# A routed decoder block on one core: a re-ordered mixer, no branch ahead of the first expert, and branch values read together

## The chip, the cores and the metric

The kernel runs on one core of one Trainium2 chip, from one launch, with all inputs and the output in the core's HBM. The metric is device microseconds (us) of one execution; the number given is the median of three. Five engines work side by side: PE (matrix products; its weight loads are a second row, PEld), DVE and ACT (element-wise work), POOL (element-wise work and some DMA issues), and SP, which only issues DMAs. Each runs its own list of instructions in order and waits at semaphores for the others.

## What is computed

One decoder block over 256 tokens of width 1024, in float32. A token mixer with two branches (a short causal convolution, and a state-space scan with 32 heads in 4 groups) is followed by a channel mixer that sends each token to 4 of 32 experts. Cut to what matters here:

```
h = rms_norm(x) * (1 + sc1) + sh1                       # sh, sc, gt: silu(c) @ w_ada + b_ada, six rows
proj = h @ w_in -> sb, sc, sx, z, xbc, dt, gate_a, gate_b
y_a = (sc * conv3(sb * sx)) @ w_sconv_out
xs, bs, cs = split(silu(conv4(xbc) + b)); dt = softplus(dt + dt_bias); a = -exp(a_log)
y   = scan(xs, dt, a, bs, cs) + d_skip * xs             # over the 256 tokens
y_b = group_rms_norm(y * silu(z)) @ w_ssm_out           # 4 groups of 512
x   = x + gt1 * ((sigmoid(gate_a) * y_a + sigmoid(gate_b) * y_b) @ w_o)
h   = rms_norm(x) * (1 + sc2) + sh2
logits = h @ w_router + b_router                        # top 4 of 32, softmax over the 4
for each expert e, over the tokens sent to it:
    gate, up = h @ w_gu[e] + b_gu[e]
    out += weight * (((clip(up) + 1) * gate * sigmoid(1.702 * gate)) @ w_down[e] + b_down[e])
out = rms_norm(x + gt2 * out) * g_final
```

## The kernel before, in words

**The mixer.** `items` is a list of projections, each a product of a 1 MB weight with the 256 normalised tokens. A weight is split into a high and a low part (`split`, L189 to L191: ACT writes the high part, POOL or DVE subtracts to get the low one) and each product is done as three (`mm3`, L193 to L196). `add(load, engines, run)` registers an item and says which engine makes the low part of its two halves; `take()` (L224) hands out the next half and at the same time issues the splits of the halves up to three further on. The order is: dt (`run_dt`, L458), 4 convolution items for B and C (`conv_pair`, L498), 8 for xs, 8 for z (`run_z`), 12 for the short convolution (`run_sb`, `run_sx`, `run_sc`), two gates, 4 of `run_ya`, 8 of `run_yb`, 6 of `run_gate`, and the output product `w_out`. The scan is cut into steps; `ssd_step` (L666) runs the steps placed at the next position, two positions per item of z and of the short convolution. `group_norm(g)` (L627) sums squares on PE, takes a reciprocal root on DVE (`rsqrt_mean`) and returns a `finish` that spreads it over the rows by a PE product.

**The loop over items** (L941 to L953) runs an item, then what the item before it left in `later`, then the row steps that `rows_here` put there, then the item's `after` hooks. A row step (`row_step`, L357) adds one of 32 slices of `w_ada` into an accumulator on DVE (L362, L364); after 8 slices a row of modulation is complete and `total` (PE, L373) and `turn` follow, one item apart.

**The experts' weights** come in pieces of 2 MB, six an expert (four of `w_gu`, two of `w_down`), through a ring of ten places. `eissue(n)` (L99) issues the pieces up to number n. Most ring places are buffers of the mixer, so the first ten pieces start as the mixer lets go of them, and piece j + 10 when the expert that read piece j is done with it. PE, ACT, DVE and POOL keep the order of the program; the order of SP's queue is laid out by the program's own scheduler, since SP is not among the engines in `MANUAL`.

**The experts** run in pairs (`expert`, L1325; `last_pair`, L1339). Expert e takes up to 64 rows (`CAP`): products `gate_up` (L1194 biases, L1198), the activation on DVE and ACT, a turn, products `down` (L1224); the pair's output is weighted and added by `combine` (L1244, L1246). Rows 65 to 96 of an expert are done in branches. Between expert e and e + 1 stands a branch on the larger of the two counts (`cnt2`), and inside it two more on the count of each (`extra_down`, `extra_gate_up`). A branch is taken on PE, ACT and DVE, each of which loads the count into a register first (`rows_of`, L1306). Ahead of expert 0 stands a branch of its own, on its count (L1135, L1317). Any rows past 96 of an expert are done at the end by `leftover`, under a branch on the largest count (`cnt_max`, L1515).

## Time and profile before

| | |
|---|---|
| median of 3 runs | 1399.8 us (1398.98 to 1400.66) |
| the profiled execution, its own time | 1405.03 us |
| its span (first to last recorded instruction) | 1403.2 us |
| mean granted PE clock | 0.971 of full speed |
| PE busy | 1309.4 us (93%), 7417 products |
| DVE / ACT / POOL busy | 550.0 / 287.2 / 91.1 us |
| bytes read from HBM | 492.45 MB, mean 352 GB/s |

The mixer takes the span up to about 450 us, the experts the rest. A row of a timeline gives the start and the length in us, the engine, the line, the operation, and in brackets how long the engine had been idle before it and what ended that. `PEq`, `ACTq`, `SPq` are the engines' sequencers (branches, register loads, DMA issues). A busy PE is not PE at its peak: the same product is shorter at the full clock than at half of it.

### The profile page before, as it was taken

What the parts mean: (1) busy time and instruction counts of PE and PEld (TensorE: products, weight loads), DVE (VectorE), ACT (ScalarE), POOL (GpSimd) and SP (SyncE); (2) the same over time, 40 slices, a digit from 0 to 9 for tenths busy, and PEclk for the clock granted to TensorE, in tenths of its full rate; (3) what the DMA queues carried; (4) which work ended last, traced back from release to release, by engine and by line L of the source; (5) the groups of instructions that cost most, each with busy time, mean ns of one, the idle gap of its engine ahead of it and who ended that gap; (6) DMA issues with size and microseconds to landing.
All of it is one profiled execution on the core that took longest, in us unless ns stands there. A gap on an engine that the chain in (4) does not pass through costs nothing. (4 is left out here: it accounts for less than half of the span.)

```text
span 1403.2 us, 18018 instructions
## 1 busy us (share of the span) xinstructions
PE 1309.4 (93%) x7417; PEld 735.8 (52%) x7417; DVE 550.0 (39%) x1026; ACT 287.2 (20%) x440; POOL 91.1 (6%) x71
## 2 busy tenths in 40 slices
PE   4899999999988999999999999999989888999995
PEld 1899998899987344344333434434423233334432
DVE  1846788976744223213212322222321213221323
ACT  1657965454433000000000000000000000000002
POOL 3682000000022000000000000000000000000000
PEclk9899999999989999999999999999999998999998
DMA  9555545568977799999999999999999999999991
GB/s 363 219 193 182 196 180 191 182 234 306 360 271 282 315 422 426 425 426 425 425 426 427 426 425 424 428 423 426 425 426 425 425 426 427 417 393 426 428 409 69
DMA packets 47977, 495.46 MB, mean 353 GB/s; under 512 B 6640, under 2 KB 6768, under 8 KB 15200
## 3 DMA queue, kind: packets, MB, share of 16 engines
q1 hardware_dynamic: 46928, 492.48, 86.0%
q8 instruction: 97, 1.59, 0.5%
q0 software_dynamic: 624, 0.53, 0.1%
q10 hardware_dynamic: 288, 0.52, 0.1%
q14 instruction: 40, 0.33, 0.1%
HBM read 492.45 MB, written 1.06 MB: 352 GB/s over the span
## 5 line engine op out<-in xcount | busy, mean ns | idle before, releaser
L1198 PE MATMUL pgu<-ring,arena 128*64 128x512 f32 x1856 | 418.0, 606 | 9.3 <-DMA ring<-in_w_gu_dram 9.2
L1198 PEld LDWEIGHTS pgu<-ring,arena 128*64 128x64 f32 x1856 | 135.0, 139 | 275.7 <-issue 257.1
L1185 DVE TENSOR_SCALAR arena<-pgu 128x512 f32<-128x512 f32 x32 | 22.1, 692 | 512.4 <-PE pgu L1198 302.3
L1224 PE MATMUL py<-ring,arena 128*64 128x512 f32 x912 | 202.8, 596 | 0.7 <-ACTq L1354 0.7
L1186 ACT ACTIVATE pgu<-arena 128x512 f32<-128x512 f32 x32 | 19.3, 602 | 732.3 <-DVE arena L1185 732.3
L1224 PEld LDWEIGHTS py<-ring,arena 128*64 128x64 f32 x912 | 62.7, 137 | 126.7 <-issue 112.4
L191 DVE TENSOR_TENSOR parts<-arena,parts 128x1024 fp32r<-128x1024 f32 x76 | 93.5, 1238 | 46.7 <-ACT parts L190 46.6
L190 ACT ACTIVATE parts<-arena 128x1024 fp32r<-128x1024 f32 x94 | 97.8, 1050 | 56.2 <-issue 15.6
L1496 POOL TENSOR_TENSOR arena<-arena 128x512 f32<-128x512 f32 x2 | 2.5, 1270 | 946.0 <-DVE arena L1246 946.0
L1244 PE MATMUL pcm<-arena 128*128 128x512 f32 x128 | 61.7, 605 | 0.9 <-DVE arena L1474 0.9
L194 PE MATMUL pc<-slot_h,parts 128*128 128x256 f32 x192 | 56.3, 293 | 2.7 <-DVE arena L514 2.7
L196 PE MATMUL pc<-slot_h,parts 128*128 128x256 f32 x192 | 55.9, 291 | 2.9 <-POOL parts L191 2.9
L1158 PE MATMUL pgat<-arena 128*128 128x128 f32 x480 | 58.5, 275 | 0.0
L1474 DVE TENSOR_TENSOR arena<-py,arena 128x512 f32<-128x512 f32 x32 | 20.6, 686 | 95.4 <-PE py L1224 80.9
L1158 PEld LDWEIGHTS pgat<-arena 128*128 128x128 f32 x480 | 56.1, 192 | 0.0
L195 PE MATMUL pc<-slot_h,parts 128*128 128x256 f32 x192 | 55.7, 290 | 0.0
L1194 PE MATMUL pgu<-bgu 128*128 128x512 f32 x64 | 24.3, 462 | 27.9 <-PEq L1320 17.5
L191 POOL TENSOR_TENSOR parts<-arena,parts 128x1024 fp32r<-128x1024 f32 x18 | 45.5, 2536 | 73.3 <-DVE row_ebuf L364 43.8
L1198 PE MATMUL pgu<-arena 128*64 128x512 f32 x192 | 43.3, 593 | 1.0 <-DMA arena<-in_w_gu_dram 0.9
L514 DVE SCALAR_TENSOR_TENSOR arena<-pc,arena 128x253 f32<-128x253 f32 (+2 forms) x72 | 33.5, 481 | 23.0 <-ACT arena L509 21.3
L1246 DVE TENSOR_TENSOR arena<-arena,pcm 128x512 f32<-128x512 f32 x64 | 39.9, 680 | 1.1 <-PE pcm L1244 1.1
L196 PEld LDWEIGHTS pc<-slot_h,parts 128*128 128x128 f32 x192 | 38.2, 199 | 3.3 <-POOL parts L191 3.3
(342 smaller groups left out, 2041.0 us busy)
## 6 DMA issues: line engine op xcount, KB each, us to landing
ring<-in_w_gu_dram SPq DMA_DIRECT2D x116, 2048.0 KB, 27.1
ring<-in_w_down_dram SPq DMA_DIRECT2D x54, 2048.0 KB, 28.0
arena<-in_w_gu_dram SPq DMA_DIRECT2D x12, 2048.0 KB, 33.0
arena<-in_w_main_dram SPq DMA_DIRECT2D x23, 1024.0 KB, 5.6
row_ebuf<-in_w_ada_dram SPq DMA_DIRECT2D x32, 512.0 KB, 4.0
arena<-in_w_down_dram SPq DMA_DIRECT2D x6, 2048.0 KB, 31.5
ring_more<-in_w_main_dram SPq DMA_DIRECT2D x9, 1024.0 KB, 6.7
arena<-in_w_gate_dram SPq DMA_DIRECT2D x8, 1024.0 KB, 7.6
```

The source lines that it names most:

```text
L190: nc.scalar.activation(hi, src, AF.Copy)
L191: lo_engine.tensor_tensor(lo, src, hi, op=ALU.subtract)
L194: nc.tensor.matmul(dst, w[0], x[0], start=first, stop=False)
L195: nc.tensor.matmul(dst, w[0], x[1], start=False, stop=False)
L196: nc.tensor.matmul(dst, w[1], x[0], start=False, stop=last)
L514: nc.vector.scalar_tensor_tensor(ts[a][:, d:], pm[:, a, 0:T - d], v2t[:, col:col + 1], ts[a][:, d:], op0=ALU.mult, op1=ALU.add)
L1158: nc.tensor.matmul(pg[:, k], h2[:, tb, k0 + k], sel[:, tb], start=(tb == 0), stop=(tb == 1))
L1194: nc.tensor.matmul(pgu[i], bias_lhs(), bias_rhs(i), start=True, stop=False)
L1198: nc.tensor.matmul(pgu[q // 2][64 * hh:64 * hh + 64], xg[:, k, s0:s0 + CAP], w[k // 2][:, k % 2, 512 * q:512 * q + 512], start=False, stop ...
L1224: nc.tensor.matmul(outs[dh][64 * cg:64 * cg + 64], aT[:, q, 64 * h:64 * h + 64], w[h][:, q, 512 * dh:512 * dh + 512], start=(h == 0 and q ...
L1244: nc.tensor.matmul(pc, pwT[:, dh, tb], ysb[:, dh], start=True, stop=True)
L1246: nc.vector.tensor_tensor(o_acc[:, tb, sl], o_acc[:, tb, sl], pc, op=ALU.add)
```

## The change

It has three parts. In the mixer: small products of a unit matrix are put behind the last three `w_ada` products and behind the turn of the modulation (`idle_products`); the copy into `rcol` goes behind `make_h`; `run_dt` is cut into five parts of which four are run one item later each; the second convolution item gets one half's subtraction on DVE (`MIXED`); `turn_dt` goes from the first xs item to the sixth; `group_norm` and its `finish` get fixed positions; one row step leaves the last `run_sc` item, one each leaves the gates (1, 1) and (2, 1), and three more stand at `run_yb`; pieces 1 to 3 of the expert weights are issued one at a time behind the gates (1, 0), (2, 0) and (2, 1). Ahead of expert 0: the register load and the branch go; `cmax` is raised by 32 above expert 0's count, so that rows past 64 of expert 0 are left to `leftover`, which shifts expert 0's positions to match. At the other branches: the counts for the outer and the two inner branches are loaded together inside `down`, in front of the branch.

```diff
--- before.py
+++ after.py
@@ -314,6 +314,13 @@
 
     smod0 = at(40, [P, 512])
     pm0 = paux("pada0", [P, 512])
+
+
+    def idle_products(nm, n):
+        t = ptr(nm, [P, P])
+        for i in range(n):
+            nc.tensor.matmul(t, ident, ident, start=True, stop=True)
+
     xps = []
     for i in range(8):
         ada_mm(pm0, i, ada0[i])
@@ -323,10 +330,13 @@
             turn_small()
         if i == 3:
             turn_x()
+        if i >= 5:
+            idle_products(f"idle{i}", 3)
     nc.vector.tensor_tensor(smod0, pm0, badar, op=ALU.add)
     mcol_p = ptr("mcol_p", [P, 4, P])
     for q in range(4):
         nc.tensor.transpose(mcol_p[:, q], smod0[:, P * q:P * q + P], ident)
+    idle_products("idle8", 14)
 
     nc.vector.tensor_copy(mcol.rearrange("p r q -> p q r"), mcol_p[:, :, 0:P:32])
     mflat = mcol.rearrange("p r q -> p (r q)")
@@ -387,9 +397,6 @@
 
         later.append(total)
 
-
-    nc.vector.tensor_copy(rcol, v1t[:, BA0:BA0 + 32].rearrange("p (r j) -> p r j", j=8))
-
     def mod_rows(r):
         src = mod_d[r]
         return bass.AP(tensor=src.tensor, offset=src.offset, ap=[[0, P], [1, D]])
@@ -455,26 +462,39 @@
     acum = at(34, [NH, T])
     dtx, dz, du, dl, dc, dtv = (at(28 + i, [NH, T]) for i in range(6))
 
+    na = const.tile([NH, 1], F32, name="na")
+
     def run_dt():
         pdt = paux("pdt", [P, T])
         proj(pdt, take(), hx)
         nc.vector.tensor_scalar(dtx, pdt[:NH], dtb, None, op0=ALU.add)
         nc.vector.scalar_tensor_tensor(dz, dtx, -1.0, dtx, op0=ALU.mult, op1=ALU.min)
         nc.scalar.activation(dz, dz, AF.Exp)
+        nc.scalar.activation(na, alog, AF.Exp)
+        later.append(dt_log)
+
+    def dt_log():
         nc.vector.tensor_scalar(du, dz, 1.0, None, op0=ALU.add)
         nc.scalar.activation(dl, du, AF.Ln)
-        na = const.tile([NH, 1], F32, name="na")
-        nc.scalar.activation(na, alog, AF.Exp)
         nc.vector.tensor_scalar(na, na, -1.0, None, op0=ALU.mult)
         nc.vector.tensor_scalar(dc, du, -1.0, None, op0=ALU.add)
         nc.vector.tensor_tensor(dc, dz, dc, op=ALU.subtract)
         nc.vector.reciprocal(du, du)
+        later.append(dt_sum)
+
+    def dt_sum():
         nc.vector.tensor_tensor(dc, dc, du, op=ALU.mult)
         nc.vector.tensor_tensor(dl, dl, dc, op=ALU.add)
         nc.vector.scalar_tensor_tensor(dtv, dtx, 0.0, dl, op0=ALU.max, op1=ALU.add)
+        later.append(dt_scan)
+
+    def dt_scan():
         nc.vector.tensor_scalar(dc, dtv, na, None, op0=ALU.mult)
         nc.vector.memset(dz, 1.0)
         nc.vector.tensor_tensor_scan(acum, dz, dc, 0.0, op0=ALU.mult, op1=ALU.add)
+        later.append(dt_parts)
+
+    def dt_parts():
         nc.vector.tensor_copy(acum_hi, acum)
         nc.vector.tensor_tensor(acum_lo, acum, acum_hi, op=ALU.subtract)
         nc.vector.tensor_copy(dsk[0:64], dsk_r[0:64, 0:NH:2])
@@ -523,15 +543,15 @@
 
     for j in range(4):
         i = 2 * j
-        add(main(28 + j), POOL2 if i else MIXED, lambda i=i: conv_pair(16 + i, [bcx[:, i], bcx[:, i + 1]]))
+        add(main(28 + j), POOL2 if i > 2 else MIXED, lambda i=i: conv_pair(16 + i, [bcx[:, i], bcx[:, i + 1]]))
     for j in range(8):
         i = 2 * j
 
         def run_xs(i=i):
             conv_pair(i, [xs[:, i], xs[:, i + 1]])
-            if i == 0:
+            if i == 10:
                 turn_dt()
-            elif i <= 8:
+            elif 2 <= i <= 8:
                 cb_group(i // 2 - 1)
 
         add(main(20 + j), POOL2, run_xs)
@@ -646,7 +666,6 @@
         return finish
 
     ssd_at = {}
-    ssd_late = []
 
     def place_ssd(pos, fn, early=False):
         fns = ssd_at.setdefault(pos, [])
@@ -660,12 +679,12 @@
         place_ssd(pos + 4, lambda hp=hp: ssd_square(hp))
         place_ssd(pos + 5, lambda hp=hp: ssd_sum(hp))
         if hp % 4 == 3:
-            place_ssd(pos + 6, lambda g=hp // 4: ssd_late.append(group_norm(g)))
+            place_ssd(pos + 6, lambda g=hp // 4, pos=pos: place_ssd(
+                pos + (7 if g == 3 else 8), group_norm(g)))
     ssd_pos = [0]
 
     def ssd_step():
-        late, ssd_late[:] = ssd_late[:], []
-        for fn in ssd_at.get(ssd_pos[0], []) + late:
+        for fn in ssd_at.get(ssd_pos[0], []):
             fn()
         ssd_pos[0] += 1
 
@@ -711,7 +730,7 @@
     for cp in range(4):
         for i, (j, run) in enumerate(((0, run_sb), (8, run_sx), (4, run_sc))):
             add(main(j + cp), DVE2, lambda run=run, cp=cp: run(cp))
-            if i:
+            if i and (cp, i) != (3, 2):
                 rows_here(1)
 
 
@@ -818,18 +837,18 @@
     for j in range(8):
         add(lambda j=j: wload(w_ssm_out[j].rearrange("p (a k) n -> p a k n", a=2)), DVE2,
             lambda j=j: run_yb(j))
-        rows_here(1)
+        rows_here(2 if j in (1, 2, 5) else 1)
         if j == 2:
             after(lambda: nc.sync.dma_start(gate1, mod_rows(0)))
     for cp in range(1, 4):
         for s in range(2):
             add(gate_load(cp, s), DVE2, lambda cp=cp, s=s: run_gate(cp, s))
-            if cp < 3:
+            if cp < 3 and s == 0:
                 rows_here(1)
             if cp == 1 and s == 0:
                 after(lambda: nc.sync.dma_start(o_acc, x[0].rearrange("(t p) d -> p t d", p=P)))
-            if cp == 2 and s == 0:
-                after(lambda: eissue(4))
+            if (cp, s) in ((1, 0), (2, 0), (2, 1)):
+                after(lambda n=(2, 3, 4)[cp + s - 1]: eissue(n))
             if cp == 3 and s == 0:
                 after(lambda: eissue(5))
             if cp == 1 and s == 1:
@@ -937,6 +956,8 @@
 
     presplit(1)
     make_h()
+
+    nc.vector.tensor_copy(rcol, v1t[:, BA0:BA0 + 32].rearrange("p (r j) -> p r j", j=8))
     presplit(3)
     for i, run in enumerate(items):
         late, later[:] = later[:], []
@@ -1131,8 +1152,10 @@
     weights(0)
     weights(1)
     nc.vector.tensor_reduce(cmax, pps[1][:, 1], axis=mybir.AxisListType.X, op=ALU.max)
+
+    nc.vector.scalar_tensor_tensor(cmax, pps[1][:, 1, 0:1], float(XCAP), cmax, op0=ALU.add,
+                                   op1=ALU.max)
     nc.vector.tensor_copy(cnt_max, cmax)
-    rows0 = nc.values_load(cnt[0:1, 0:1], engines=IF_ENGINES, min_val=0, max_val=T)
     mixer.close()
 
 
@@ -1305,23 +1328,23 @@
     def rows_of(src, e):
         return nc.values_load(src[0:1, e:e + 1], engines=IF_ENGINES, min_val=0, max_val=T)
 
-    def over(src, e):
-        return rows_of(src, e) > CAP
-
     w_of = {}
 
 
+    def overflow_rows(e):
+        return [rows_of(*v) for v in ([(cnt2, e), (cnt, e), (cnt, e + 1)] if e else [(cnt, 1)])]
+
     def overflow(e, rows):
-        w_of[e + 1] = load_expert(e + 1)
-        if e < 0:
-            with tc.If(rows > CAP):
-                extra_gate_up(0, w_of[0][0], ux)
-        else:
-            with tc.If(rows > CAP):
-                with tc.If(over(cnt, e)):
-                    extra_down(e, w_of[e][1], ux)
-                with tc.If(over(cnt, e + 1)):
-                    extra_gate_up(e + 1, w_of[e + 1][0], ux)
+        if e + 1 not in w_of:
+            w_of[e + 1] = load_expert(e + 1)
+        with tc.If(rows[0] > CAP):
+            if e == 0:
+                extra_gate_up(1, w_of[1][0], ux)
+                return
+            with tc.If(rows[1] > CAP):
+                extra_down(e, w_of[e][1], ux)
+            with tc.If(rows[2] > CAP):
+                extra_gate_up(e + 1, w_of[e + 1][0], ux)
 
     def expert(e, xg, s0, fill, py, cgs):
         w = w_of[e]
@@ -1332,8 +1355,8 @@
         aT = turn(e, u)
         fill[1]()
         rows = []
-        down(w[1], aT, py, cgs, lambda: rows.append(rows_of(cnt2, e)))
-        overflow(e, rows[0])
+        down(w[1], aT, py, cgs, lambda: rows.extend(overflow_rows(e)))
+        overflow(e, rows)
 
 
     def last_pair(a, xg, fills, py):
@@ -1349,15 +1372,12 @@
                 aTa = turn(a, u)
                 w_of[b] = load_expert(b)
             fills[i][1]()
-        down(w_of[a][1], aTa, py, (0, 1))
+        rows = []
+        down(w_of[a][1], aTa, py, (0, 1), lambda: rows.extend(overflow_rows(a)))
         aTb = turn(b, u, at(place["ysb"], [P, 4, P]))
-        with tc.If(over(cnt2, a)):
-            with tc.If(over(cnt, a)):
-                extra_down(a, w_of[a][1], ux)
-            with tc.If(over(cnt, b)):
-                extra_gate_up(b, w_of[b][0], ux)
+        overflow(a, rows)
         down(w_of[b][1], aTb, py, (1, 0))
-        with tc.If(over(cnt, b)):
+        with tc.If(rows[2] > CAP):
             extra_down(b, w_of[b][1], ux)
 
 
@@ -1367,6 +1387,8 @@
         for i, base in enumerate((ids, 2 * ids, ids + P, 2 * ids + P)):
             nc.vector.tensor_scalar(pos_of[:, i], posm.rearrange("p t e -> p (t e)"),
                                     float(-base), None, op0=ALU.add)
+        nc.vector.tensor_scalar(pos_of[:, :, 0:2 * NE:NE], pos_of[:, :, 0:2 * NE:NE], float(XCAP),
+                                None, op0=ALU.add)
         for e in range(NE):
             w = load_expert(NE + e)
             for b in range(2):
@@ -1426,7 +1448,7 @@
         bias_product(pb, tb, hh)
         add_bias(pb, tb, hh)
 
-    overflow(-1, rows0)
+    w_of[0] = load_expert(0)
     for pr in range(NE // 2):
         a, b = 2 * pr, 2 * pr + 1
         last = pr + 1 == NE // 2
```

## Rows read from the trace of the kernel before

**Rows 1.** A stretch: busy us per engine (count), granted clock, DMA share, GB/s.
```profile
1085.00:1120.00 35.00, 31.16 (x134) 10.03 (x132) 7.59 (x19) 1.20 (x2) 0.00 (x0) 1.00 1.00 425
```

**Rows 2.** Timeline of PE: first products of two experts, a pair apart, and an overflow branch.
```profile
591.72 0.70 PE L1194 MATMUL pgu<-bgu 128*128 128x512 f32 x2 [0.46 <-PEq L1320]
645.17 0.70 PE L1194 MATMUL pgu<-bgu 128*128 128x512 f32 x2 [0.51 <-PEq L1320]
...
1184.35 2.40 PE L1266 MATMUL pgx<-ring,arena 128*32 128x512 f32 x16 [2.31 <-DMA ring<-in_w_gu_dram]
```

**Rows 3.** Waits of PE from 460 to 1390 us: us in total, times, longest.
```profile
PE pgu L1194 <- PEq L1320: 17.5, 25, 2.5
PE pgu L1198 <- DMA ring<-in_w_gu_dram: 9.2, 7, 2.3
```

**Rows 4.** A stretch of expert 0, columns as in rows 1.
```profile
454.00:460.00 6.00, 6.00 (x19) 1.91 (x20) 0.00 (x0) 0.00 (x0) 0.00 (x0) 0.61 0.00 0
```

**Rows 5.** Timeline of PE in the first part of the mixer.
```profile
29.03 1.94 PE L311 MATMUL pada<-arena 128*32 128x512 f32 x8 [1.44 <-DMA arena<-in_w_ada_dram]
...
34.87 0.58 PE L194 MATMUL pdt<-slot_h,parts 128*128 128x256 f32 x1 [1.97 <-ACT slot_h L431]
...
52.18 0.39 PE L196 MATMUL pc<-slot_h,parts 128*128 128x256 f32 x1 [1.80 <-POOL parts L191]
...
65.00 0.36 PE L194 MATMUL pc<-slot_h,parts 128*128 128x256 f32 x1 [2.68 <-DVE arena L514]
```

**Rows 6.** Timeline there of ACT, DVE and POOL.
```profile
39.95 2.56 DVE L191 TENSOR_TENSOR parts<-ring_more,parts 128x1024 fp32r<-128x1024 f32 x1 [0.87 <-ACT parts L190]
41.39 3.39 POOL L191 TENSOR_TENSOR parts<-arena,parts 128x1024 fp32r<-128x1024 f32 x1
45.09 0.42 ACT L463 ACTIVATE arena<-arena 32x256 f32<-32x256 f32 x1 [2.92 <-DVE arena L462]
...
48.65 1.99 ACT L190 ACTIVATE parts<-arena 128x1024 fp32r<-128x1024 f32 x2
```

**Rows 7.** Timeline of PE and DVE at two group norms and a row total.
```profile
217.27 0.71 PE L638 MATMUL pb<-ident,gn_r 128*128 128x128 f32 x4 [2.14 <-DVE gn_r L160]
...
278.88 1.28 DVE L364 SCALAR_TENSOR_TENSOR row_ebuf<-row_ebuf,arena 128x1024 f32<-128x1024 f32 x1
280.55 0.61 PE L630 MATMUL pn<-arena,slot_bc 128*128 128x1 f32 x4 [2.03 <-DVE slot_bc L625]
...
285.46 1.84 PE L373 MATMUL pr<-arena,row_ebuf 128*128 128x1 f32 x16
```

**Rows 8.** Timeline of ACT and PE at the last gates.
```profile
391.84 1.06 ACT L190 ACTIVATE parts<-arena 128x1024 fp32r<-128x1024 f32 x1 [8.28 <-DMA arena<-in_w_gate_dram]
...
398.12 3.57 PE L373 MATMUL pr<-arena,row_ebuf 128*128 128x1 f32 x16 [4.63 <-DVE row_ebuf L364]
...
401.55 3.60 PE L931 MATMUL pc<-arena 128*128 128x32 f32 x16
```

**Rows 9.** Stretches in the convolution items and after the last gates, columns as in rows 1.
```profile
66.00:72.00 6.00, 6.00 (x40) 6.00 (x39) 4.43 (x10) 5.02 (x8) 5.26 (x3) 0.72 0.29 87
...
402.00:408.00 6.00, 6.00 (x29) 6.00 (x30) 1.69 (x4) 0.00 (x0) 0.00 (x0) 0.50 0.90 319
```

**Rows 10.** Timeline of DVE and PE ahead of expert 0, and PE at a later expert.
```profile
447.68 0.69 DVE L919 TENSOR_TENSOR arena<-pgat,arena 128x512 f32<-128x512 f32 x1 [0.20 <-PE pgat L1067]
...
452.93 1.19 PE L1194 MATMUL pgu<-bgu 128*128 128x512 f32 x2 [5.29 <-PEq L1317]
454.06 16.20 PE L1198 MATMUL pgu<-ring,arena 128*64 128x512 f32 x64
...
592.36 14.26 PE L1198 MATMUL pgu<-ring,arena 128*64 128x512 f32 x64
```

**Rows 11.** Lines 1306 and 1320 on PE's sequencer: ns min/median/max, starts.
```profile
L1306 PEldq TENSOR_LOAD <-arena x40: 296/304/322, 474.4 to 1381.2; - x40
...
L1320 PEldq COMPARE_BRANCH  x30: 70/342/6452, 477.0 to 1331.6; - x30
```

## The prediction

> **What bounds the kernel now.** I read the page's slices first: PE is nearly full throughout, DMA only from about 490 us on. Then a table of stretches, the waits of PE, and the timelines of the places where PE stood still.
>
> In the experts' part two limits lie close together. A pair of experts takes PE 645.17 - 591.72 = 53.45 us, 26.7 an expert [rows 2]. An expert's weights are six pieces of 2048 KB, 12.58 MB, and the DMA engines, wholly busy, move 425 GB/s [rows 1]: 29.6 us. So PE eats the store of loaded pieces, 2.9 us an expert, and the store lasts until about 1030 us. From there to 1187 us PE waits for pieces: 9.2 us in gate and up products [rows 3] and 2.3 in an overflow branch, the last such wait, which ends at 1184.35 [rows 2]; 11.5 in all. The rest of that second overflow branch gives DMA time to refill, and to the end PE waits for no piece again. Hence the end is set by the DMA stream up to 1184 us, and by PE after that.
>
> The stream begins when expert 0 lets go of its pieces. From 454 to 460 us DMA moves nothing at all [rows 4]: all ten places are full and PE has only begun. Whatever makes PE begin expert 0 earlier by x moves stream and PE by x alike, and the end with them. So the mixer's length counts in full, and in the mixer PE is the engine that sets it: I add up where it stands still or runs at half clock.
>
> **The change part by part.**
>
> *Front, up to 40 us.* [...] Three small products now stand behind each of the last three groups and 14 behind the turn, in the 1.97 us for which PE waits for the first normalised tokens [rows 5]. Should the clock stay high, the turn, the last group and the dt products shorten by up to 3 us, but the next weight half is ready no sooner than ACT and POOL make it, so little of that gets through. Should it stay low, the 14 products fill more than the gap, by up to 2 us. The rcol copy leaves the chain, 0.2 us. I take 0.9 us saved, bounds -2 and 3.
>
> *Convolution items, 40 to 75 us.* PE waits 1.80 us at 52.18 for a low part, and 2.68 us at 65.00 for the DVE taps of an older item [rows 5]; the clock falls behind both: 0.72 over six microseconds behind the second [rows 9], 6 x 0.28 = 1.7 us of work, and somewhat less behind the first, so 3 in all. The first comes from ACT: its split at 48.65 stands behind the dt exponentials and logarithm, which begin at 45.09 [rows 6]. In the new order the logarithm goes to the next item, so this split can begin near 46, and the low half is DVE's. The second wait comes from the dt chain on DVE, now spread over four items, behind each item's taps. Waits and clock losses make 7.5 us. What is late next is DVE itself, which gets a subtraction more, 2.56 us beside POOL against 1.2 alone [rows 6]. I take 4.0; bounds 0 and 7.5.
>
> The row of DVE at 39.95 lies beside POOL's at 41.39, 3.39 us long [rows 6]. [...]
>
> *Group norms and row steps.* PE waits 2.14 us at 217.27 for the root; with finish one position later (half an item, some 3 us) that is gone. At 280.55 it waits 2.03 us for DVE; the row step at 278.88, 1.28 us, stands right ahead of that and is the one that leaves the last run_sc item [rows 7]. 0.75 us of the wait stay. 2.1 + 1.3 = 3.4; the clock loss behind it, about as large as the one above, may go too. Bounds 1.3 and 5.0. The three row steps added at run_yb, 1.3 us each, lie on a DVE with room: hidden; their 0.5 MB each lie where DMA is nearly full, at most 1.2 us each if a weight comes late for it.
>
> *Last gates.* A gate's weight lands late, behind pieces of 2 MB: ACT stands 8.28 us to 391.84. That holds up the sigmoid and the row step behind it, and PE waits 4.63 us for the total at 398.12 [rows 8]. The total then takes 3.57 us at the low clock, against 1.84 for the same 16 products at 285.46 [rows 7, 8]; the router's 16 take 3.60, about 1.8 too many by that ratio; and the gate behind them runs at 0.50 to about 411 us [rows 9], some 2.6 us more. 4.6 + 1.7 + 1.8 + 2.6 = 10.7. Now the last row step comes two items earlier, and pieces 1 to 3, issued in one go ahead of that weight, are spread out: each that now goes behind it takes 2.1 MB, 4.9 us at 425 GB/s, out of its way. The weight may still be late for a us. I take 9.5; bounds 3 and 10.7.
>
> *Ahead of expert 0.* PE ends its last gather at 452.93 - 5.29 = 447.64 and begins expert 0 at 452.93, behind the branch (5.29 us of it idle); its inputs are there when DVE's second addition ends, 447.68 + 0.69 = 448.4 [rows 10]. Without load and branch PE waits for that, or at worst for DVE's last reads of the old accumulators, some 1.5 us later: 3.0 to 4.5 us saved. Expert 0's 64 products took 16.20 at a clock of 0.61 [rows 4] against 14.26 later [rows 10]: 1.9 more if the clock holds, and 0.5 at the bias products. 3.8 + 2.4 = 6.2; bounds 3.0 and 6.9.
>
> *The other branches.* Each gets two loads more on PE's sequencer, 2 x 0.304 = 0.6 us and a few register operations, say 0.9 [rows 11], and as many on ACT and DVE. They stand in down with 12 float32 products queued in front and behind; PE's sequencer is then ahead of the products, and the branch itself waits up to 6.5 us for them [rows 11]. The 0.46 us of idle at the next expert [rows 2] stays. Cost nothing; without that cover 0.9 a branch. In the two overflows the inner loads go: about 0.5 us a branch, of which only those past 1184 us count, 0.5, and as much in the last pair: 1.2 in all, bounds 0 and 2.4.
>
> Sum: 0.9 + 4.0 + 3.4 + 9.5 + 6.2 + 1.2 = 25.2. The profiled execution took 1405.0 (span 1403.2 and 1.8 around it), so 1379.8 for it; it is 5.2 above the median of the runs, 1399.8, and I forecast by that: **1374.6 us**. All bounds at their good end give 35.5, all at the bad end about 5.
>
> **Rivals.**
> (a) *The stalls come back.* Split, DVE or late weights take the place of what goes in the mixer. For it: DVE is busy there and DMA at 0.90 [rows 9]. What can't come back is the branch (5), the row step (1.3) and half the gate stall (5): 11 us, **1389**.
> (b) *The stream doesn't follow.* If the ring, not expert 0, set the stream's start, only what lies past 1184 us would count: 1.2 us, **1398.6**. Against it: the six empty microseconds [rows 4].
> (c) *The branch pays, slower.* Three loads and a nested body could make PE stand at each of 30 branches; 0.46 us is usual, 2.5 the longest [rows 2, 3]. With g more a branch the loss is 30 g less the 11.5 us in which PE waits for pieces anyway; it passes my gain from g = (25.2 + 11.5) / 30 = 1.2 us. At the 2.0 of the longest, 60 - 11.5 - 25 = 23.3 more: **1423**. Against it: the 25 waits sum to 17.5 us [rows 3], so the long ones are few.
> [...]
> (d) *The leftover pass runs*, if expert 0 has more than 64 rows: 32 experts of 29.6 us, about 947 more. Against it: behind the branch at 452.93 the bias products of expert 0 follow with no overflow product between [rows 10].
>
> **Chances.** Forecast 0.76, (a) 0.14, (b) 0.03, (c) 0.06, (d) 0.01. Range: 1365 (35.5 saved) to 1391 (takes in (a)); 1.5 in 10 is left out. About 0.2%, 2.8 us, is what a measurement can tell. Faster 0.90, same 0.03, slower 0.07.
>
> **What would show it.** Expert 0's first product near 425 to 430 us instead of 452.93, with under 2 us of idle before it and the clock at 1.00; no low clock at the last gates; no PE wait at the second group norm; waits for PEq ahead of L1194 still near 0.5 us; DMA moving again from about 435 us instead of 460; last waits for pieces about 25 us earlier. Wrong: a mixer that ends less than 12 us sooner, or waits at the branches grown past 1 us.

## The result, and the profile after

The changed kernel takes 1369.4 us (median of 4 runs, 1368.7 to 1369.7) against 1399.6 for the kernel before (1399.0 to 1400.7) on the same chip: a ratio of 0.978, interval 0.977 to 0.980. It is 30.1 us faster; 25.2 were forecast, and 1369.4 lies inside the range.

Where the time went is read off the first PE product of each stage (for expert 0, the first with weights; its start is called the mark of expert 0 below). The profiled execution of before was some 5 us above its median, so a second profile of the unchanged kernel (run e4 below) stands beside it. Lengths in us, from the timelines of PE:

| stretch | before | before again | after |
|---|---|---|---|
| start to the first convolution product (end of the front) | 40.0 | 40.2 | 39.7 |
| convolution items | 81.5 | 80.9 | 73.7 |
| gate, scan and third-part items, the group norms among them | 195.1 | 198.1 | 190.1 |
| second third-part items and the gates, to the output product | 96.8 | 94.9 | 86.2 |
| output product and routing, to expert 0 | 40.7 | 40.2 | 35.7 |
| expert 0 to PE's last wait for a piece in the second overflow | 730.3 | 729.1 | 726.2 |
| from there to the end | 218.9 | 215.2 | 216.4 |
| span | 1403.2 | 1398.6 | 1367.9 |

Against the profile of before that the prediction used, 28.6 us of 35.3 lie ahead of expert 0; against the second profile, 28.9 of 30.7. From expert 0 on, the changed kernel is 1.9 us shorter than the second profile and 6.7 shorter than the first. The excess of the first profile was 3.7 us behind the last wait (a stretch of ten microseconds there has a granted clock of 0.88, in the other 1.00) and about 1 ahead of it.

The page of the changed kernel, its span and busy times (share of the span, number of instructions):

```profile
span 1367.9 us, 18272 instructions
...
PE 1296.2 (95%) x7463; PEld 725.8 (53%) x7463; DVE 555.7 (41%) x1028; ACT 286.4 (21%) x439; POOL 89.4 (7%) x70
```

PE was 93% busy of 1403.2, that is 93.8 us idle; now 71.7. So 22 us of the gain are idle time of PE, and 13 are busy time: 46 more matmuls in 13 us less, since products run at the high clock that ran at the low one (mean granted clock 0.988, 0.971 before).

PE's waits in the mixer (us in total, times, longest), from 34 to 425 us of the changed kernel:

```profile
PE pc L196 <- POOL parts L191: 1.2, 1, 1.2
PE pgat L1088 <- DVE arena L1148: 0.9, 1, 0.9
PE pn L650 <- DVE slot_bc L645: 0.8, 1, 0.8
PE po L195 <- POOL parts L191: 0.6, 1, 0.6
```

The waits of 4.63, 2.68, 2.14, 2.03 and 1.80 us [rows 5, 7, 8] are gone or under 1.3. At the stretches that answer to [rows 9] and [rows 4] (columns as there), behind the dt chain, at the last gates, and at expert 0's first products:

```profile
66.00:72.00 6.00, 6.00 (x53) 6.00 (x52) 5.89 (x7) 3.20 (x6) 6.00 (x3) 1.00 0.69 220
...
374.00:380.00 6.00, 6.00 (x54) 6.00 (x53) 4.44 (x6) 2.18 (x3) 0.00 (x0) 1.00 1.03 396
...
424.00:430.00 6.00, 6.00 (x34) 2.71 (x34) 2.80 (x13) 0.00 (x0) 0.00 (x0) 1.00 0.79 284
```

The granted clock is 1.00 in all three, where it stood at 0.72, 0.50 and 0.61 before; 53 products instead of 40 fit into the first. DMA no longer stops at expert 0 (0.79 instead of 0.00).

In the timeline of PE (start, length, line, operation, in brackets the wait and its releaser) expert 0 and a table load behind it:

```profile
424.80 0.71 PE L1217 MATMUL pgu<-bgu 128*128 128x512 f32 x2
425.44 13.95 PE L1221 MATMUL pgu<-ring,arena 128*64 128x512 f32 x64
```
```profile
439.40 1.28 ACT L1209 ACT_TABLE_LOAD   x1 [18.00 <-DVE arena L1208]
...
441.54 1.12 PE L1105 MATMUL pbd<-arena 32*128 32x512 f32 x2 [1.58 <-ACT arena L1101]
```

The 5.29 us ahead of expert 0 [rows 10] are gone and its 64 products take 13.95 for 16.20. New is the place of ACT's table load, 439.40: it now stands behind ACT's wait for its input, PE waits 1.58 us for what follows, and the clock falls to 0.72 in the six microseconds behind. In before it ran right behind ACT's branch, 22 us ahead of the activation that uses it:

```profile
446.75 1.28 ACT L1186 ACT_TABLE_LOAD   x1 [2.76 <-ACTq L1317]
```

At the branches, a usual and a long wait, and the sums from 430 us on that answer to [rows 3]:

```profile
536.38 1.15 PE L1217 MATMUL pgu<-bgu 128*128 128x512 f32 x2 [2.16 <-PEq L1340]
...
594.33 0.70 PE L1217 MATMUL pgu<-bgu 128*128 128x512 f32 x2 [0.34 <-PEq L1340]
...
1151.55 3.23 PE L1289 MATMUL pgx<-ring,arena 128*32 128x512 f32 x16 [2.98 <-DMA ring<-in_w_gu_dram]
```
```profile
PE pgu L1217 <- PEq L1340: 20.9, 25, 2.4
PE pgu L1221 <- DMA ring<-in_w_gu_dram: 6.6, 5, 1.6
PE pgx L1289 <- DMA ring<-in_w_gu_dram: 3.2, 2, 3.0
```

The usual wait fell from 0.46 to 0.34, but seven are of 2.0 to 2.4 us where three were; in sum 3.4 us more. Six of the seven lie before 1151 us, where PE waits for pieces anyway: those waits fell from 11.5 to 9.8.

### The profile page after: what moved, and what is told of

Read it like the earlier page. It is cut to its first block, busy times and chain, and to the rows that moved or that the text cites. A ratio compares the mean times of both kernels' runs of the same rounds, so it can differ in the third digit from the quotient of the medians.

```text
span 1367.9 us, 18272 instructions
## 1 busy us (share of the span) xinstructions
PE 1296.2 (95%) x7463; PEld 725.8 (53%) x7463; DVE 555.7 (41%) x1028; ACT 286.4 (21%) x439; POOL 89.4 (7%) x70
## 3 DMA queue, kind: packets, MB, share of 16 engines
HBM read 492.45 MB, written 1.06 MB: 361 GB/s over the span
## 5 line engine op out<-in xcount | busy, mean ns | idle before, releaser
L1221 PE MATMUL pgu<-ring,arena 128*64 128x512 f32 x1856 | 411.9, 600 | 6.6 <-DMA ring<-in_w_gu_dram 6.6
L1221 PEld LDWEIGHTS pgu<-ring,arena 128*64 128x64 f32 x1856 | 131.0, 138 | 270.4 <-issue 258.3
L1496 DVE TENSOR_TENSOR arena<-py,arena 128x512 f32<-128x512 f32 x32 | 20.6, 686 | 94.9 <-PE py L1247 80.9
L196 PE MATMUL pc<-slot_h,parts 128*128 128x256 f32 x192 | 54.4, 283 | 1.2 <-POOL parts L191 1.2
L194 PE MATMUL pc<-slot_h,parts 128*128 128x256 f32 x192 | 54.7, 285 | 0.0
L195 PE MATMUL pc<-slot_h,parts 128*128 128x256 f32 x192 | 54.3, 283 | 0.0
L1217 PE MATMUL pgu<-bgu 128*128 128x512 f32 x64 | 23.3, 445 | 25.2 <-PEq L1340 20.9
L1237 ACT ACTIVATE arena<-pact 128x512 f32<-128x512 f32 x32 | 19.1, 597 | 89.3 <-PE pact L1235 89.3
## 6 DMA issues: line engine op xcount, KB each, us to landing
arena<-in_w_down_dram SPq DMA_DIRECT2D x6, 2048.0 KB, 28.6
```

The source lines that it names most:

```text
L194: nc.tensor.matmul(dst, w[0], x[0], start=first, stop=False)
L195: nc.tensor.matmul(dst, w[0], x[1], start=False, stop=False)
L196: nc.tensor.matmul(dst, w[1], x[0], start=False, stop=last)
L1217: nc.tensor.matmul(pgu[i], bias_lhs(), bias_rhs(i), start=True, stop=False)
L1221: nc.tensor.matmul(pgu[q // 2][64 * hh:64 * hh + 64], xg[:, k, s0:s0 + CAP], w[k // 2][:, k % 2, 512 * q:512 * q + 512], start=False, stop ...
```

## The experiments

The kernels of each of the three groups ran on one chip together; a ratio is to before in the same group. The changed kernel did not run in them again: "above the changed kernel" is against its 1369.4 us. Runs of the kernel before went from 1395 to 1406 us there, so effects under 3 us are read from the traces' marks.

### One part of the change at a time

**e1, the mixer's new order alone.** This is the changed kernel with everything behind the routing weights as before, the first branch and the loads inside the branches included. The core of the edit, against the changed kernel:

```diff
+    rows0 = nc.values_load(cnt[0:1, 0:1], engines=IF_ENGINES, min_val=0, max_val=T)
...
-        down(w[1], aT, py, cgs, lambda: rows.extend(overflow_rows(e)))
-        overflow(e, rows)
+        down(w[1], aT, py, cgs, lambda: rows.append(rows_of(cnt2, e)))
+        overflow(e, rows[0])
...
-    w_of[0] = load_expert(0)
+    overflow(-1, rows0)
```

> Only the mixer's part of the change; the branch ahead of expert 0 and the nested register loads stay. Theory (what PE saves before expert 0 counts in full): the two profiles put first products of w_out 23.7 us earlier, so 1399.6 - 23 = 1376 to 1378, and expert 0 still begins behind 5 us of idle at a low clock. Rival (the stream's start has its own limit, the ring): the mixer alone gives less than 12 us, over 1387.

Measured: 1374.9 us, ratio 0.983 (0.980 to 0.986). Expert 0 begins at 428.5, 25.5 us earlier than in before, and the time falls by 24.3. The gain of the mixer comes through in full; the rival falls. The idle time at the branch is 3.07 us, not the 5 expected:

```profile
427.42 1.19 PE L1215 MATMUL pgu<-bgu 128*128 128x512 f32 x2 [3.07 <-DVEq L1338]
```

So 23.6 of the 25.5 us lie ahead of the output product, and some 2 are a shorter wait at a branch that is still there (3.07 for 5.29; the last section shows what the trace has ahead of the longer one). The step from here to the whole change is 3.1 us at expert 0 and 4.1 in the span.

**e2, no branch in front of expert 0, alone:**

```diff
...
-    rows0 = nc.values_load(cnt[0:1, 0:1], engines=IF_ENGINES, min_val=0, max_val=T)
...
-                with tc.If(over(cnt, e)):
-                    extra_down(e, w_of[e][1], ux)
+                if e > 0:
+                    with tc.If(over(cnt, e)):
+                        extra_down(e, w_of[e][1], ux)
...
-    overflow(-1, rows0)
+    w_of[0] = load_expert(0)
```

> Only the branch ahead of expert 0 goes (its rows past 64 left over to the end); mixer and other branches as before. Theory: 3.0 to 4.5 us of idle and up to 2.4 of low clock, 5 to 7 us faster, 1393 to 1395. Rival (PE waits for the same inputs and the table load anyway): under 3 us, over 1396.5.

Measured: 1398.2 us, ratio 0.998 (0.996 to 1.000): a miss. Nine of its ten runs lie between 1389.7 and 1401.4 us (median 1397.7); one took 3355.4, has no trace and is not explained. The timeline of PE:

```profile
448.83 13.95 PE L1199 MATMUL pgu<-ring,arena 128*64 128x512 f32 x64
...
1175.62 1.92 PE L1267 MATMUL pgx<-ring,arena 128*32 128x512 f32 x16 [0.47 <-DMA ring<-in_w_gu_dram]
...
1219.62 12.04 PE L1199 MATMUL pgu<-ring,arena 128*64 128x512 f32 x48 [3.54 <-DMA ring<-in_w_gu_dram]
...
1248.89 0.70 PE L1195 MATMUL pgu<-bgu 128*128 128x512 f32 x2 [2.42 <-PEq L1321]
```

The step itself does what was forecast: expert 0 begins 5.3 us earlier, its products take 13.95, and the wait in the second overflow ends at 1175.62, 7.8 before that of e4. ACT's table load is out of the way (it ran at 443.75, ahead of ACT's wait). But then PE waits once more for a piece, 3.54 us, and 2.42 at a branch, and those 6 us take most of it back. So the time fits the rival's, not its mechanism. The long branch wait is one of seven here (before has three); why a piece is late at 1219 us wasn't settled, nor whether the faster runs have that wait.

**e3, the three loads together, alone:**

```diff
...
-        down(w[1], aT, py, cgs, lambda: rows.append(rows_of(cnt2, e)))
-        overflow(e, rows[0])
+        down(w[1], aT, py, cgs, lambda: rows.extend(overflow_rows(e)))
+        overflow(e, rows)
...
```

> Only the counts of the inner branches read together with the outer; mixer and first branch as before. Theory: 0.9 us more of register loads a branch is hidden behind queued products, 1 to 2 us faster, 1397.5 to 1399. Rival (the loads make PE stand, 0.9 a branch): PE's waits for pieces take up 11 us of 28, so 10 to 16 us slower, 1410 to 1416.

Measured: 1400.6 us, ratio 1.001 (1.000 to 1.003): no gain where 1 to 2 us were expected, and the slower rival is excluded. Its waits at the branch:

```profile
PE pgu L1194 <- PEq L1320: 21.0, 25, 2.3
```

The usual wait is shorter, as in the whole change, but seven are long; the sum is 3.5 us above the 17.5 of [rows 3]. At the usual branch (0.31 to 0.34 us here, 0.46 to 0.55 in before) two loads more on a sequencer cost nothing.

**e4, before again**, nothing changed, for a second profile.

> The kernel before once more, for its profile: the first profiled execution took 1405.0 us, 5.2 above the median, so one of its stages was longer than usual. Theory: the extra lies in the experts' part (branches that waited 2 us rather than 0.5); the mixer's stages agree within 1 us. Rival: the mixer's stages differ by several us from one execution to the next, and the comparison of stages by one profile is that uncertain.

Measured: 1400.3 us, span 1398.6; its marks are in the table above. Up to the output product (413.4 and 414.1 us) the two profiles agree within a microsecond. Stage by stage they do not: the gate, scan and third-part items took 3.0 us more here, the stretch to the output product 1.9 less. So the rival holds for single stages, and a stage's gain by one profile is known to some 2 or 3 us.

### The mixer's parts, taken back one by one

**a1, the last gates as before:**

```diff
-        rows_here(2 if j in (1, 2, 5) else 1)
+        rows_here(2 if j == 1 else 1)
...
-            if cp < 3 and s == 0:
+            if cp < 3:
                 rows_here(1)
...
-            if (cp, s) in ((1, 0), (2, 0), (2, 1)):
-                after(lambda n=(2, 3, 4)[cp + s - 1]: eissue(n))
+            if cp == 2 and s == 0:
+                after(lambda: eissue(4))
```

> The changed kernel with the row steps at the gates and the issue of pieces 1 to 3 (three in one go behind gate (2, 0)) as before. Theory: the late weight and the low clock at the last gates return, 9 to 11 us slower than the changed kernel, 1378 to 1381. Rival (they were due to where the mixer stood then, not to the order): under 3 us, below 1372.5.

Measured: 1383.1 us, ratio 0.989 (0.985 to 0.993), 13.6 above the changed kernel, more than expected; the mark of expert 0 is 11.1 later. ACT and PE in its timeline, and the stretch behind (columns as in rows 1):

```profile
380.79 1.06 ACT L190 ACTIVATE parts<-arena 128x1024 fp32r<-128x1024 f32 x1 [10.38 <-DMA arena<-in_w_gate_dram]
...
387.07 3.57 PE L383 MATMUL pr<-arena,row_ebuf 128*128 128x1 f32 x16 [6.72 <-DVE row_ebuf L374]
```
```profile
390.00:396.00 6.00, 6.00 (x29) 6.00 (x30) 2.64 (x5) 0.00 (x0) 0.36 (x1) 0.50 0.72 259
```

The whole chain of [rows 8] is back: the late weight (10.38 us of ACT), the wait for the row step, the total at half speed (3.57), and a clock of 0.50 behind. In the changed kernel the same places read:

```profile
372.75 1.06 ACT L190 ACTIVATE parts<-arena 128x1024 fp32r<-128x1024 f32 x1 [2.27 <-DMA arena<-in_w_gate_dram]
374.49 1.84 PE L383 MATMUL pr<-arena,row_ebuf 128*128 128x1 f32 x16
...
382.13 1.87 PE L950 MATMUL pc<-arena 128*128 128x32 f32 x16
```

**a2, the dt chain in one piece, POOL's part of the splits as before:**

```diff
-        later.append(dt_log)
...
-        add(main(28 + j), POOL2 if i > 2 else MIXED, lambda i=i: conv_pair(16 + i, [bcx[:, i], bcx[:, i + 1]]))
+        add(main(28 + j), POOL2 if i else MIXED, lambda i=i: conv_pair(16 + i, [bcx[:, i], bcx[:, i + 1]]))
...
-            if i == 10:
+            if i == 0:
                 turn_dt()
```

> The changed kernel with run_dt in one piece, the second convolution item's subtractions both on POOL and turn_dt in the first xs item, as before. Theory: the two waits of 1.8 and 2.7 us and the clock losses behind them return, 6 to 8 us slower, 1375.5 to 1377.5. Rival (the small products hold the clock, which was the larger part): 2 to 4.5 us, 1371.5 to 1374.

Measured: 1379.3 us, ratio 0.986 (0.982 to 0.990), 9.9 above, more than expected; expert 0 is 7.8 later, all of it by 121 us. Both waits of [rows 5] are back to the hundredth:

```profile
52.13 0.39 PE L196 MATMUL pc<-slot_h,parts 128*128 128x256 f32 x1 [1.80 <-POOL parts L191]
...
64.94 0.36 PE L194 MATMUL pc<-slot_h,parts 128*128 128x256 f32 x1 [2.68 <-DVE arena L521]
```

**a3, the group norms and row steps as before.** With this edit slice 24's row step goes into an accumulator from which the third modulation row has not yet been totalled, so that row's values differ, and the experts' counts may. Up to expert 0 the time does not depend on them, and the first overflow begins 302.4 us behind expert 0, in the changed kernel 302.3.

```diff
...
-            place_ssd(pos + 6, lambda g=hp // 4, pos=pos: place_ssd(
-                pos + (7 if g == 3 else 8), group_norm(g)))
+            place_ssd(pos + 6, lambda g=hp // 4: ssd_late.append(group_norm(g)))
...
-            if i and (cp, i) != (3, 2):
+            if i:
                 rows_here(1)
...
-        rows_here(2 if j in (1, 2, 5) else 1)
+        rows_here(2 if j in (1, 2) else 1)
```

> The changed kernel with group_norm's steps and the row step of the last run_sc item as before. Theory: waits of 2.1 and 1.3 us and part of a clock loss return, 3.4 to 5 us slower, 1373 to 1374.5. Rival (DVE has the room by now, since its dt chain moved): under 1.5 us, below 1371.

Measured: 1377.7 us, ratio 0.985 (0.981 to 0.989), 8.2 above, more than expected; expert 0 is 6.5 later. Both waits return, and behind the second a low clock:

```profile
209.26 1.22 PE L658 MATMUL pb<-ident,gn_r 128*128 128x128 f32 x4 [2.13 <-DVE gn_r L160]
...
275.22 0.61 PE L650 MATMUL pn<-arena,slot_bc 128*128 128x1 f32 x4 [2.02 <-DVE slot_bc L645]
```
```profile
276.00:282.00 6.00, 6.00 (x41) 6.00 (x40) 5.58 (x16) 5.97 (x6) 0.00 (x0) 0.72 0.68 259
```

**a4, no idle products in the front:**

```diff
-        if i >= 5:
-            idle_products(f"idle{i}", 3)
...
-    idle_products("idle8", 14)
```

> The changed kernel without the small products of the unit matrix. Theory: the front is held by the weight split and the normalised tokens, not by the clock, so 0 to 1 us slower, 1369 to 1370.5. Rival (the clock they hold is worth its whole loss): 2.5 to 4 us slower, 1372 to 1373.5.

Measured: 1370.4 us, ratio 0.980 (0.976 to 0.983), 1.0 above. The convolution items begin 0.5 later than in the changed kernel, but the later stages, from 75.7 us to the output product, begin within 0.1 us of each other. Two rows of it:

```profile
28.85 1.55 PE L311 MATMUL pada<-arena 128*32 128x512 f32 x8 [1.44 <-DMA arena<-in_w_ada_dram]
...
34.70 0.58 PE L194 MATMUL pdt<-slot_h,parts 128*128 128x256 f32 x1 [2.39 <-ACT slot_h L435]
```

The clock that the idle products hold is real (from 28 to 34 us it is 1.00 with them, 0.61 without, and 0.55 in before, and the last w_ada group takes 1.06 and 1.55 us), but the dt products begin at 34.7 in both kernels: they wait for ACT's normalised tokens. Expert 0 is 0.9 later here, but not by the front: PE waits 0.78 us for DVE right ahead of its bias product, which it does not in the changed kernel.

By the marks of expert 0 the first three parts are worth 11.1 + 7.8 + 6.5 = 25.4 us, against 25.5 for the whole mixer alone (e1), some 2 of them at the branch. So they overlap little, and the idle products add nothing that lasts. By the median times the three cost more, 31.7 us. The profiled execution is the fastest of the four in each of a1 to a3; by the spans it ends 8.5, 5.2 and 6.4 us after that of the changed kernel. What the other executions spend 1 to 6 us more on has no trace and stays open.

### Does expert 0's start set the end?

Sixty small products on PE (no part of the result) delay it at one place of the changed kernel: ahead of expert 0, ahead of expert 10, and ahead of expert 28, which lies behind the last wait for a piece.

```diff
+        if e == 0:   # 10, 28
+            t = ps2.tile([P, P], F32, tag="tr", name="wait")
+            for _ in range(30):
+                nc.tensor.matmul(t, ident, ident, start=True, stop=True)
         pgu = gate_up(e, w[0], xg, s0)
```

**d0:**

> The changed kernel with 30 idle products (some 7 us of PE) ahead of expert 0's first product. Theory (PE's start of expert 0 moves stream and PE alike): the end moves by the whole delay, 6.5 to 7.5 us later, about 1376.5. Rival (the stream sets its own start): the 10.7 us in which PE waits for pieces later take it up, under 1.5 us, below 1371.

**d10:**

> The same 30 products ahead of expert 10, in the stretch where PE eats the store of loaded pieces. Theory (the stream decides until the second overflow, at about 1152 us): PE waits that much less for pieces later, the end moves by 0 to 2 us, 1369.5 to 1371.5. Rival (PE alone sets the end): 7 us later, 1376.5.

**d28:**

> The same 30 products ahead of expert 28, behind the last wait for a piece. Theory (from there PE sets the end): 6.5 to 7.5 us later, about 1376.5. Rival (the stream sets the end to the last): under 1.5 us, below 1371.

Their delays in the timeline of PE, of d0, d10 and d28:

```profile
424.72 6.86 PE L1354 MATMUL wait<-ident 128*128 128x128 f32 x60
```
```profile
701.04 8.56 PE L1354 MATMUL wait<-ident 128*128 128x128 f32 x60 [2.21 <-PEq L1340]
```
```profile
1251.12 6.94 PE L1354 MATMUL wait<-ident 128*128 128x128 f32 x60 [0.33 <-PEq L1340]
```

d0 took 1380.1 us (ratio 0.985, 0.982 to 0.988), 10.7 above the changed kernel. Its 6.86 us move expert 0 by 6.5 and the last wait for a piece by 7.6, as the theory has it. Behind that wait 4.2 more are lost: two long branch waits (2.26 and 2.25) fall there where the changed kernel has one, and three stretches of ten microseconds have a granted clock of 0.83 to 0.85 (1.00 in the changed kernel). The rival, a stream that doesn't follow, falls.

d28 took 1379.2 us (ratio 0.985, 0.982 to 0.987), 9.8 above: the delay and one more long branch wait (1.96, ahead of expert 29). So 6.94 + 1.96 = 8.9 us behind the last wait for a piece cost no less than themselves.

d10 took 1374.9 us (ratio 0.984, 0.980 to 0.987), 5.5 above; 0 to 2 were expected. PE's waits for pieces of the ring shrank from 9.8 to 3.4 us, as expected, but the stream itself lost time. The stretch of the first overflow (columns as in rows 1) in d10, and in the changed kernel:

```profile
780.00:820.00 40.00, 36.45 (x144) 12.09 (x138) 12.92 (x27) 1.20 (x2) 0.00 (x0) 0.91 0.88 356
```
```profile
780.00:820.00 40.00, 39.69 (x182) 14.21 (x179) 9.36 (x22) 1.80 (x3) 0.00 (x0) 1.00 1.01 425
```

Overflow products eat no new pieces. With PE late, pieces are let go of late: SP's next issue in the first overflow comes at 780.50, in the changed kernel at 772.61, and DMA falls to 356 GB/s: 40 x (1 - 356 / 425) = 6.5 us of stream lost. So there is a second place, besides expert 0, at which PE holds the stream up; in the changed kernel, where DMA stays at 425 there, it isn't reached.

### A version that takes away what is new

**i1, the table load ahead of expert 0**, by one small sigmoid behind the routing weights:

```diff
     weights(1)
+    nc.scalar.activation(nwt[:, 2, 0:1], eps, AF.Sigmoid)
```

> The changed kernel with one small sigmoid on ACT behind the routing weights, so that the table load of 1.28 us, which now stands between expert 0's products and its activation, is done while PE runs those products. Theory: the 1.58 us wait of PE at expert 0 goes and the low clock behind it (0.72 over six us, 1.7 us), 2 to 3.5 us faster, 1366 to 1367.5. Rival (the table is loaded a second time, or the wait is hidden by the pieces): within 0.7 us of 1369.4.

```profile
420.89 1.28 ACT L1154 ACT_TABLE_LOAD   x1
...
439.74 1.12 PE L1105 MATMUL pbd<-arena 32*128 32x512 f32 x2 [0.30 <-DVE arena L1211]
```
```profile
442.00:448.00 6.00, 6.00 (x27) 2.03 (x28) 4.33 (x14) 0.60 (x1) 0.00 (x0) 1.00 1.01 433
```

Measured: 1367.3 us (five runs, 1365.6 to 1371.2), ratio 0.978 (0.975 to 0.980). In the trace the load runs at 420.89 while PE gathers, PE's wait falls from 1.58 to 0.30, and the clock behind it is 1.00 for 0.72. By the time it can't be told from the changed kernel (0.977 to 0.980). From expert 0 to the last wait for a piece it takes 724.0 us against 726.1, but so do a1 and a2 (724.6 and 724.8), whose load stands where the changed kernel has it. So the local gain is shown, a gain in the whole is not. It has the lowest median here, and beats before beyond doubt.

## Why the prediction was right, and where its sizes were off

**The path.** The step that carried it, that the end follows expert 0's start, is shown: expert 0 to the last wait in the second overflow took 724 to 730 us in thirteen of the fourteen profiles, whatever the mixer took (733 in d10, whose delay lies inside), and 215 to 219 from there on in all but e2, d0 and d28, which have the waits or the delay named above in it. d0 moved both. One part of the path fails: by the prediction PE has a store of pieces to eat until about 1030 us, so that, as d10's expectation took from it, a late PE costs nothing there; d10 lost 5.5 us. The six empty microseconds of [rows 4], the argument against rival (b), were the right row to read; with the earlier start that pause shrank to a dip (0.79), and the second pause behind expert 0 went too.

**Convolution items: 4.0 forecast, 7.2 to 7.8 measured.** This is the term that was most mis-sized. The working found 7.5 (two waits, two clock losses) and took about half, since DVE, with a subtraction more, might be late next. It was not. The new split and its two halves in the timeline of the changed kernel, ACT, DVE, POOL:

```profile
45.30 1.99 ACT L190 ACTIVATE parts<-arena 128x1024 fp32r<-128x1024 f32 x2
46.37 1.23 DVE L191 TENSOR_TENSOR parts<-arena,parts 128x1024 fp32r<-128x1024 f32 x1 [1.53 <-ACT parts L190]
47.36 2.49 POOL L191 TENSOR_TENSOR parts<-arena,parts 128x1024 fp32r<-128x1024 f32 x1 [2.79 <-ACT parts L190]
```

The split begins at 45.30 instead of 48.65, and the moved subtraction takes 1.23 us, not 2.56 [rows 6] (the 1.2 alone that the prediction takes from there does not stand in them; by the page of before the 76 such subtractions on DVE take 1.24 us in the mean): POOL starts when ACT has its high part ready, 0.24 us before DVE ends. The 2.56 us of before lie beside POOL's subtraction ahead of those in rows 6: that one ends at 41.43 us, and DVE's, begun at 39.95, ends 1.1 us after it. In the changed kernel the same pair does the same (POOL ends at 41.23, DVE runs from 39.74 to 42.31). What sets the length of two that lie beside each other, no run takes apart.

```profile
39.05 2.38 POOL L191 TENSOR_TENSOR parts<-ring_more,parts 128x1024 fp32r<-128x1024 f32 x1 [0.92 <-DMA row_ebuf<-in_w_ada_dram]
```

**Group norms and row steps: 3.4 forecast, 5.0 measured** against the first profile, 8.0 against the second, and 6.5 by the mark of a3. Both waits went as said (2.14 to none, 2.03 to 0.85); what was left out of the value is the clock behind the second, which a3 shows at 0.72 and which the prediction named as a loss that "may go too".

**Last gates: 9.5 forecast**, 10.6 and 8.7 by the two profiles, 11.1 by a1. All four pieces of the chain are right: wait, total, router, gate. The weight is still 2.27 us late for ACT, which PE doesn't feel.

**Ahead of expert 0: 6.2 forecast.** The stretch is 5.0 us shorter (4.5 against the second profile) and expert 0's products 2.25 shorter, 7 in all. Not all of it is the branch's: e1, which keeps the branch, waits 3.07 us there and not 5.29, and its products take 15.02, so by e1 the branch is worth 3.1 and 1.1. The table load takes some of it back, a cost that the forecast had not seen; it does not come with the missing branch as such, since in e2, a4 and d0, which have no branch there either, the load is out of the way. Taken alone (e2), the step gained 1 us of time, within noise, because late waits behind 1175 us took it back.

**Front: 0.9 forecast, 0.3 to 0.5 measured**, and by a4 nothing of the idle products' part is left at 75.7 us. No run shows the 0.9, or the 3 us at its good end: from 28 to 34 us the clock is 1.00 for 0.55, and the last w_ada group takes 1.06 us for 1.94 [rows 5], yet the first dt product begins at 34.66 for 34.87.

**Other branches: 1.2 gained forecast; not there.** The added loads are hidden, as argued, and the 0.46 us became 0.34 rather than staying. But long waits went from three to seven, and the sum rose by 3.4. Rival (c) had the right place and the wrong size: 3.4 / 30 = 0.1 us a branch, where 1.2 would have been needed. The traces show a packet of kind instruction ahead of each of the 96 long waits (last section).

The rivals: (a) at 1389, no stall came back in the mixer beyond 1.2 us; (b) excluded by e1 and d0; (c) excluded; (d) no leftover pass ran. And one size fell out: the forecast's base was the median, with 5.2 taken off the profiled execution's sum; e4 shows that the 5 us lay in the experts' part, where only the 1.2 of the other branches stood, so hardly anything was taken off a term twice.

## What to carry to other kernels

Where one engine is full and feeds a stream, find the place where the stream stands still for it, and count everything ahead of that place in full; an engine that looks full may still lose time there to short waits and to products at the lower clock behind each. Here 4.48 us of waits cost 7.8 (a2) and 6.72 cost 11.1 (a1), so when a wait goes, count the slow products too, unless the next late thing has a row. And when a branch goes, look at what other engines did while they stood behind it (here a table load): it may move to where it is first needed, as this one did, from 22 us ahead of its user to right ahead of it, though not in e2, a4 and d0. The 30 branches of this kernel had a lottery in them: a few instructions more or fewer ahead of them changed which ones wait 2 us (3 to 9 of them), so read a gain of that size from marks that lie ahead of the branches.

## What the runs showed of the hardware

**Ahead of each long branch wait the trace has a packet of kind instruction.** At each of the other branches PE stands 0.3 to 0.5 us, but at 3 to 9 of them some 2 us (1.5 to 3.6). The DMA view of the trace shows what differs. Queues of the changed kernel in the 3.0 us ahead of the product at 536.38 (a wait of 2.16), and ahead of the one at 594.33 (0.34):

```profile
q1 hardware_dynamic: 80, 1.26, 99.8%
q8 instruction: 1, 0.02, 2.2%
```
```profile
q1 hardware_dynamic: 87, 1.26, 98.9%
```

In the 14 profiles together, from 440 us on, PE has 96 waits over 1.4 us that the profile puts down to a branch (93 at the other branches, 3 ahead of expert 0). Each of the 96 ends 2.6 to 3.1 us after the start of a packet of q8, kind instruction, and so does each of 12 waits of 0.6 to 1.4 us at the other branches. Of 252 waits there under 0.6 us, 6 do. Ahead of expert 0 this holds in both profiles of before and in e3 (5.29, 4.79 and 4.80 us), but not in e1 (3.07). That PE waits for what these packets bring is a reading of this order in time; no run takes them away.

Which branches wait so long moved with the code ahead of them. In the changed kernel they stand ahead of experts 4, 5, 10, 15, 20, 21 and 27. The 60 products of d28 leave these where they are and add expert 29, behind them. Those of d10 leave 4, 5 and 10 and move the rest to 13, 18, 19, 23, 28 and 29. Those of d0 move all, to 2, 3, 9 and then the same six as in d10. In before they are the same three in both profiles (ahead of experts 1, 10 and 21). Ahead of the last wait for a piece they cost nothing that shows: the changed kernel has six there for the three of before, and its stretch from expert 0 to that wait takes 726.2 us for 730.3 and 729.1. Behind it the one added in d28 (1.96 us) stands in full in the 9.8 that the run lost, alone as large as some of the edits above.

**A table load stood behind its user's wait in one run and ahead of it in another.** In the changed kernel it ran behind ACT's wait for the input of the activation that needs it (18.00 us idle, then 1.28 of load), not in the idle time before. This is not always so: in d0, whose ACT code is the same, it ran ahead of a wait of 23.37 us:

```profile
421.25 1.28 ACT L1209 ACT_TABLE_LOAD   x1
445.91 0.60 ACT L1209 ACTIVATE pgu<-arena 128x512 f32<-128x512 f32 x1 [23.37 <-DVE arena L1208]
```

The wait instruction that ACT's sequencer runs ahead of the load lasted 18.29 us in the changed kernel and 0.02 in d0, so the wait for the input stands ahead of the load in one and behind it in the other. In a4 and e2 it is as in d0. What decides between the two stays open. A small activation of the same function put earlier moved the load from 439.40 to 420.89 us, where ACT was free (i1).
